# First chunk of a one-core trunk layer: q summed while h is made, k and v taken forward, modulation sums on ScalarE

## The chip, the cores and the metric

One core of one Trainium2 chip runs the whole kernel in one launch; the host only lays the arrays out. The metric is the device time in microseconds (us). Engines are named as in the profile: PE is TensorE (PEld its weight loads), DVE VectorE, ACT ScalarE, POOL GpSimd, and SP SyncE, which here issues every DMA.

## The reference

One layer on 2048 tokens of width 1024, in float32:

```python
mod = silu(c) @ w_ada + b_ada
shift, scale, gate = split(mod)                  # 1024 each
h = rms_norm(x, norm_g) * (1 + scale) + shift
u = h @ w_in                                     # 1024 x 5632
glu_in, gate_a, q, k, v, gate_b, m_a, m_b = split(u)
y_a = conformer_conv_branch(glu_in, gate_a, ...) # GLU, causal depthwise conv 31, LayerNorm, swish, proj
q = head_rms_norm(q, q_gain); k = head_rms_norm(k, k_gain)   # 8 heads x 64
o = stick_breaking_attention(q, k, v)
y_b = (o * silu(gate_b)) @ w_sb_out
y = sigmoid(m_a) * y_a + sigmoid(m_b) * y_b
x = x + gate * (y @ w_out)
```

The changed part makes `h`, the columns of `w_ada` for shift and scale, and `q`, `k`, `v` of the first chunk.

## The kernel before

The tokens lie reversed, and are worked on in four chunks of 512 in the order 3, 2, 1, 0 (`ORDER`). Every large product is made of three float32r matmuls (high part by high part, high by low, low by high), so each weight and each activation is split: ScalarE copies the high part (`whi`, `hhi`), and GpSimd or VectorE subtracts it for the low part (`wlo`, `hlo`). A weight panel of 128 x 1024 comes in two halves of 128 x 512 through the two-buffer tile `wl` (`split_into`, lines 105 to 111): DMA, ScalarE copy, subtraction, for which GpSimd is the default.

**h of a chunk.** `xn_pair` (line 329) loads two blocks of 128 tokens, sums squares on ScalarE, computes a reciprocal root in ten small VectorE steps (`rsqrt`) and scales `xt` on VectorE (line 342). `x_block` transposes 128 x 128 pieces on TensorE (line 127). `modulate` (line 353) then makes `hf` = scale * x + shift on ScalarE (line 359), the high part on ScalarE for the first chunk and on VectorE for the others (lines 364 and 366), and the low part on GpSimd or VectorE (line 367). `h_half` does this for half a chunk.

**The first chunk (chunk 3).** For each of the eight 128-row slices of the model width, `mod_col` (line 225) multiplies two rows-blocks of `w_ada` with silu(c) and sums them on VectorE, two one-element VectorE sums add the bias and the gain (lines 408 and 410, `b_s` and `a_s`), and the slice of h is made. Right behind it go the matmuls of this slice into the PSUM tiles of q, heads 0 to 3 (group 0). Those of group 1 (heads 4 to 7) come after, from weights kept in tiles `w1h` and `w1l`. Then h of chunks 2, 1 and 0 is made, and q of group 0 of these chunks is begun.

**q, k and v.** There are six groups of four heads: 0 and 1 are q, 2 and 3 k, 4 and 5 v. `nat_tile` makes one half (256 tokens) of a group in a chunk: 2 token blocks x 8 slices x 3 = 48 matmuls of 128 x 256 into a `pd` PSUM tile, of which there are five. For q and k, ScalarE squares each head with a running sum (line 272), `head_norm` computes the root on VectorE and scales into `qn` (line 287), and `transposed` turns two heads at a time on TensorE, splits the result into `qhi` and `qlo` (one buffer each, lines 306 and 307, k at 302 and 303) and stores four pieces. For v, `v_store` splits (lines 318 and 319) and stores eight pieces.

**What sets the order.** A scheduler orders each engine's instructions by priority in program order, within dependences and buffers; each engine then runs its list in order, and SP issues the DMAs in order too. From the first `glu` on, TensorE's order is pinned. The depthwise convolution's 204 VectorE steps wait in a list; after each output tile `tick` gives out `RATE` of them (2.6), as well as the norms and transposes put off by `later`. The q and k transposes take `qhi` and `qlo` from the pool `cvp`, which is opened after all h is made; so those of the first chunk's q wait until then. All of k is made in `qk_group(2, True)` and `qk_group(3, True)`, v in `v_block(4)` and, in the LayerNorm stage, `v_group(5)`, in which each tile also moves the LayerNorm one step on (`next(ln)`). Attention follows, with the merge gates as filler on TensorE, and then the output projection.

Of the kernel before, what the change touches and what calls it, by code (L numbers as in the profile page):

```python
# [8 lines left out]
F32 = mybir.dt.float32  # L9
# [9 lines left out]
P = 128  # L19
SEQ = 2048  # L20
D = 1024
# [11 lines left out]
NXT = 7  # L33
NWA = 4
RATE = 2.6
# [15 lines left out]
def trunk_kernel(  # L51
# [130 lines left out]
    with ExitStack() as s1:  # L182
# [74 lines left out]
        def qk_group(grp, isk, chunks=ORDER, w2=None, ps0=None):  # L257

            w2 = w2 or ps0 or [piece(w_qkv[grp, i]) for i in range(2)]
            h4 = (grp % 2) * 4  # L260
            dst = kst_d if isk else qst_d
            for b in chunks:
# [3 lines left out]
                for half in range(2):  # L266
                    ps = ps0[half] if ps0 else nat_tile(pd, w2, b, half)
# [25 lines left out]
        def transposed(qn, pr, dst, h4, b, isk):  # L293
# [5 lines left out]
            hi = cvp.tile([P, CH], F32R, tag="qhi", name="qhi", bufs=1)  # L299
            lo = cvp.tile([P, CH], F32R, tag="qlo", name="qlo", bufs=1)  # L300
# [13 lines left out]
        def v_store(ps, st, h4, b, half):  # L314
# [7 lines left out]
            for i in range(4):  # L322
                nc.sync.dma_start(vst_d[h4 + i][b][:, 2 * half:2 * half + 2, :], s2[:, i])

# [51 lines left out]
        with tc.tile_pool(name="hx", reuse_waits="tile", bufs=1) as hx:  # L376
            g0 = ORDER[0]
            w2_q1 = [(hx.tile([P, D], F32R, name=f"w1h{i}"), hx.tile([P, D], F32R, name=f"w1l{i}"))
                     for i in range(2)]
# [6 lines left out]
            for o in range(0, D, CH):  # L386
# [5 lines left out]
            xs += xn_pair(4 * g0 + 2, hx, NXT, True)  # L392
            ba = load_const(b_ada, 24, "ba")
            ng = load_const(norm_g, KC, "ng")
            ba1 = sm.tile([P, KC], F32, name="ba1", bufs=1)
            nc.vector.tensor_scalar(out=ba1, in0=ba[:, KC:2 * KC], scalar1=1.0, scalar2=None,
                                    op0=ALU.add)
            w2_q0 = []
            qk_ps = [[pd.tile([P, 2, 256], F32, tag="pd", name="pd") for _ in range(2)]
                     for _ in range(2)]  # L400
            for kc in range(KC):
                for j in (8 + kc, kc):
                    mod_col(j, ca, hx.tile([P, D], F32, tag="wa", name="wa", bufs=NWA))
                if kc < 2:
                    w2_q0.append(load_piece(wpa, w_qkv[0, kc]))
                elif kc in (4, 5):
                    split_into(w_qkv[1, kc - 4], *w2_q1[kc - 4])
                nc.vector.tensor_tensor(out=b_s[:, kc:kc + 1], in0=mod[:, kc:kc + 1],
                                        in1=ba[:, kc:kc + 1], op=ALU.add)
                nc.vector.scalar_tensor_tensor(out=a_s[:, kc:kc + 1], in0=mod[:, 8 + kc:9 + kc],  # L410
                                               scalar=ba1[:, kc:kc + 1], in1=ng[:, kc:kc + 1],
                                               op0=ALU.add, op1=ALU.mult)
                modulate(x_block(xs, kc), hx.tile([P, CH], F32, tag="hf", name="hf", bufs=6),
                         g0, 0, kc, (1, 1),
                         nc.gpsimd if kc < KC - 1 else nc.vector)
                for half in range(2):
                    for i in range(2):
                        nat_mm(qk_ps[0][half], w2_q0, g0, half, i, kc,
                               kc == 0 and i == 0, kc == KC - 1 and i == 1)
            for kc in range(KC):  # L420
                for half in range(2):
                    for i in range(2):
                        nat_mm(qk_ps[1][half], w2_q1, g0, half, i, kc,
                               kc == 0 and i == 0, kc == KC - 1 and i == 1)
            for o in (0, 2):
                h_half(ORDER[1], o, hx, NXT, ())
            qk_group(0, False, ORDER[:1], ps0=qk_ps[0])
            for o in (0, 2):
                h_half(ORDER[2], o, hx, NXT, (0, 4))
            qk_group(1, False, ORDER[:1], ps0=qk_ps[1])  # L430
# [3 lines left out]
        with tc.tile_pool(name="hz", reuse_waits="tile", bufs=1) as hz:  # L434
# [6 lines left out]
            gain = load_const(q_gain, 1, "gain")  # L441
            gk = load_const(k_gain, 1, "gk")
            nc.vector.tensor_tensor(out=gain, in0=gain, in1=gk, op=ALU.mult)


        with tc.tile_pool(name="cvp", reuse_waits="tile", bufs=2, side="right") as cvp:
# [121 lines left out]
            qk_group(1, False, ORDER[1:])  # L568
            silu_block(B_GA + 1, ga_d[1])
            glu(2)  # L570
            qk_group(2, True)
            v_block(4)
            glu(3)
            qk_group(3, True)
# [521 lines left out]
```

## Time and profile before

| | |
|---|---|
| runs | 1952.85, 1944.73, 1953.7 us (median 1952.85) |
| profiled execution | 1947.37 us, span 1945.6 us, mean granted clock 0.993 |
| PE busy over the span | 94% |
| first glu matmul | 136.46 us after the start |
| last TensorE wait ahead of the dense stage ends | 157.4 us |
| first attention matmul | 825.4 us |
| data moved | 206.88 MB |

A row of a timeline gives start, length, engine, line of the kernel, operation, output and inputs by the program's names, shapes and, in brackets, the idle time before it with what ended it. A row of waits gives who waited for whom, the total in us, the number of waits and the longest. L12 is line 12 of the kernel before.

### The profile page before, as it was taken

What the parts mean: (1) busy time and instruction counts of PE and PEld (TensorE: products, weight loads), DVE (VectorE), ACT (ScalarE), POOL (GpSimd) and SP (SyncE); (2) the same over time, 40 slices, a digit from 0 to 9 for tenths busy, and PEclk for the clock granted to TensorE, in tenths of its full rate; (3) what the DMA queues carried; (4) which work ended last, traced back from release to release, by engine and by line L of the source; (5) the groups of instructions that cost most, each with busy time, mean ns of one, the idle gap of its engine ahead of it and who ended that gap; (6) DMA issues with size and microseconds to landing.
All of it is one profiled execution on the core that took longest, in us unless ns stands there. A gap on an engine that the chain in (4) does not pass through costs nothing.

```text
span 1945.6 us, 27211 instructions
## 1 busy us (share of the span) xinstructions
PE 1823.4 (94%) x9612; PEld 1517.2 (78%) x9612; DVE 1248.5 (64%) x1947; ACT 809.5 (42%) x1988; POOL 667.6 (34%) x739
## 2 busy tenths in 40 slices
PE   5889999999999989999998999999989889999999
PEld 4777898998988977777776777676767667888887
DVE  6864678787787445267776767676777797333341
ACT  3761122231221122266666666666667664010100
POOL 6441111011011144356465656455655551010100
PEclk9999999999999999999999999999999999999999
DMA  7335114052142444423232323131313246453532
GB/s 246 135 107 176 43 28 136 17 167 78 45 140 71 152 146 156 145 90 88 62 89 63 92 66 91 57 95 58 103 55 101 69 152 205 138 153 101 162 97 77
DMA packets 115290, 206.88 MB, mean 106 GB/s; under 512 B 15185, under 2 KB 27473, under 8 KB 115154
## 3 DMA queue, kind: packets, MB, share of 16 engines
q1 hardware_dynamic: 115154, 205.14, 33.8%
q8 instruction: 76, 1.25, 0.3%
q14 instruction: 60, 0.49, 0.1%
HBM read 133.78 MB, written 71.30 MB: 105 GB/s over the span
## 4 chain that ended last, share of the span: by engine, by line
PE 59%; DVE 16%; POOL 11%; issue 6%; DMA 5%; ACT 3%; SPq 1%; DVEq 0%; POOLq 0%; ACTq 0%
PE pd L122 33%; PE po L122 9%; POOL w L818 7%; PE p L122 7%; DVE sc L811 6%; PE av L122 4%; PE pT L127 3%; PE z L122 3%; DVE tlo L843 2%; POOL wlo L110 1%; DVE sc L815 1%; DMA gt<-ga 1%; ACT z L806 1%; DVE hhi L366 1%; DMA wl<-in_w_out_dram 1%
## 5 line engine op out<-in xcount | busy, mean ns | idle before, releaser
L818 POOL TENSOR_TENSOR w<-w,sc 128x512 f32<-128x512 f32 (+1 forms) x320 | 361.5, 1131 | 328.6 <-DVE sc L811 243.3
L122 PE MATMUL pd<-hhi,whi 128*128 128x512 f32 x1024 | 411.9, 402 | 0.0
L122 PE MATMUL pd<-hhi,wlo 128*128 128x512 f32 x1024 | 402.3, 393 | 0.0
L122 PE MATMUL pd<-hlo,whi 128*128 128x512 f32 x1024 | 401.7, 392 | 0.0
L110 POOL TENSOR_TENSOR wlo<-wl,whi 128x512 fp32r<-128x512 f32 x92 | 135.6, 1484 | 462.4 <-ACT whi L109 462.1
L811 DVE TENSOR_TENSOR_SCAN sc<-z,sc,w 128x512 f32<-128x512 f32 x192 | 244.0, 1276 | 53.1 <-ACT z L806 52.5
L805 ACT ACTIVATE w<-z 128x512 f32<-128x512 f32 (+1 forms) x320 | 171.8, 537 | 142.9 <-PE z L122 117.9
L122 PEld LDWEIGHTS pd<-hhi,wlo 128*128 128x128 f32 x1024 | 193.0, 189 | 41.9
L122 PE MATMUL pd<-whi,hhi 128*128 128x256 f32 x736 | 214.9, 292 | 8.1 <-DVE qn L287 8.1
L122 PEld LDWEIGHTS pd<-hhi,whi 128*128 128x128 f32 x1024 | 195.2, 191 | 33.8
L122 PE MATMUL pd<-whi,hlo 128*128 128x256 f32 x736 | 213.0, 291 | 8.5 <-POOL hlo L367 8.3
L122 PEld LDWEIGHTS pd<-hlo,whi 128*128 128x128 f32 x1024 | 193.6, 189 | 34.3
L122 PE MATMUL pd<-wlo,hhi 128*128 128x256 f32 x736 | 212.6, 289 | 0.2 <-POOL wlo L110 0.2
L122 PE MATMUL z<-kt,q 128*128 128x512 f32 (+2 forms) x640 | 195.9, 387 | 12.3 <-DVE sc L811 10.1
L842 ACT CAST thi<-pT 128x512 fp32r<-128x512 f32 (+1 forms) x320 | 165.1, 526 | 92.1 <-PE pT L127 88.7
L843 DVE TENSOR_TENSOR tlo<-pT,thi 128x512 fp32r<-128x512 f32 (+1 forms) x320 | 184.5, 596 | 13.4 <-ACT thi L842 11.0
L127 PE MATMUL pT<-ident,w 128*128 128x128 f32 x1088 | 174.8, 275 | 12.3 <-POOL w L818 12.1
L127 PEld LDWEIGHTS pT<-ident,w 128*128 128x128 f32 x1088 | 137.1, 140 | 49.3 <-POOL w L818 19.6
L806 ACT ACTIVATE z<-z 128x512 f32<-128x512 f32 (+1 forms) x320 | 171.5, 536 | 0.0
L122 PE MATMUL av<-tlo,vt 128*128 128x512 f32 (+1 forms) x320 | 126.1, 394 | 34.3 <-DVE tlo L843 30.5
L122 PEld LDWEIGHTS pd<-whi,hlo 128*128 128x128 f32 x736 | 143.8, 196 | 11.8 <-POOL hlo L367 11.2
L122 PEld LDWEIGHTS pd<-whi,hhi 128*128 128x128 f32 x736 | 144.9, 197 | 9.2 <-DVE qn L287 8.5
(274 smaller groups left out, 2994.3 us busy)
## 6 DMA issues: line engine op xcount, KB each, us to landing
wl<-in_w_in_dram SPq DMA_DIRECT2D x64, 256.0 KB, 2.9
wa<-in_w_ada_dram SPq DMA_DIRECT2D x24, 512.0 KB, 5.6
xt<-in_x_n_dram SPq DMA_DIRECT2D x16, 512.0 KB, 5.9
vst<-st SPq DMA_DIRECT2D x64, 128.0 KB, 1.9
kt<-kst SPq DMA_DIRECT2D x32, 256.0 KB, 2.8
vt<-vst SPq DMA_DIRECT2D x32, 256.0 KB, 2.8
q<-qst SPq DMA_DIRECT2D x32, 256.0 KB, 2.9
q<-qst SPq DMA_DIRECT2D x64, 128.0 KB, 3.1
```

What stands on the lines that cost most here:

```text
L110: (lo_eng or nc.gpsimd).tensor_tensor(out=lo[:, s], in0=wl, in1=f(hi[:, s]), op=ALU.subtract)
L122: i = nc.tensor.matmul(*a, **k)
L127: i = nc.tensor.transpose(*a)
L366: nc.vector.tensor_copy(hi, hf)
L805: nc.scalar.activation(out=w[:, lo:], in_=z[:, lo:], func=AF.Sigmoid, scale=HD ** -0.5)
L806: nc.scalar.activation(out=z[:, lo:], in_=z[:, lo:], func=AF.Sigmoid, scale=-HD ** -0.5)
L811: nc.vector.tensor_tensor_scan(out=s[:, 1:], data0=z, data1=w, initial=s[:, 0:1], op0=ALU.mult, op1=ALU.bypass)
L815: nc.vector.tensor_tensor_scan(out=s[:, lo + 1:], data0=z[:, lo:], data1=tri[:, :CH - lo], initial=1.0, op0=ALU.mult, op1=ALU.max)
L818: nc.gpsimd.tensor_tensor(out=w[:, lo:], in0=w[:, lo:], in1=s[:, lo:CH], op=ALU.mult)
L842: nc.scalar.copy(out=thi[:, :n], in_=pT[:, :n])
L843: nc.vector.tensor_tensor(out=tlo[:, :n], in0=pT[:, :n], in1=f(thi[:, :n]), op=ALU.subtract)
```

## The change

For the first chunk, both q groups are summed slice by slice while its h is made. Their norms no longer go through `qk_group` but through a new function `norm_at_once`, which squares a whole 128 x 512 PSUM tile on ScalarE, sums it by heads with one VectorE reduce, and runs `head_norm` and both transposes at once, with `qhi` and `qlo` in the pool `hx`. Then come k of the first chunk (groups 2 and 3) and its v (groups 4 and 5), each with its weights loaded for this use alone, between the four half chunks of h of chunks 2 and 1. Later, k and v of the other three chunks are made with the weights loaded a second time. The sums `a_s` and `b_s` are ScalarE instructions. `NXT`, the buffers for x blocks, goes from 7 to 6, and `RATE` from 2.6 to 2.9. `gain` is loaded at the start.

```diff
-NXT = 7
+NXT = 6
-RATE = 2.6
+RATE = 2.9
+        def norm_at_once(pss, grp, b, pool):
+
+            ssq = sm.tile([P, 4, 4], F32, tag="ssq", name="ssq")
+            qn = qp.tile([P, 4, 4, HD], F32, tag="qn", name="qn", bufs=2)
+            for half in range(2):
+                sq = pool.tile([P, CH], F32, tag="sqv", name="sqv", bufs=1)
+                nc.scalar.activation(out=sq, in_=pss[half].rearrange("p t c -> p (t c)"),
+                                     func=AF.Square)
+                nc.vector.tensor_reduce(
+                    out=ssq[:, 2 * half:2 * half + 2].rearrange("p t h -> p (t h)"),
+                    in_=sq.rearrange("p (n d) -> p n d", d=HD), axis=AX.X, op=ALU.add)
+            head_norm(pss, ssq, qn)
+            for pr in range(2):
+                transposed(qn, pr, kst_d if grp >= 2 else qst_d, (grp % 2) * 4, b, grp >= 2, pool)
...
-            w2_q1 = [(hx.tile([P, D], F32R, name=f"w1h{i}"), hx.tile([P, D], F32R, name=f"w1l{i}"))
-                     for i in range(2)]
+            def hx_piece(src, tag, lo_eng=None):
+                hi = hx.tile([P, D], F32R, tag=tag, name="whx", bufs=4)
+                lo = hx.tile([P, D], F32R, tag=tag, name="wlx", bufs=4)
+                split_into(src, hi, lo, lo_eng)
+                return hi, lo
...
-            nc.vector.tensor_scalar(out=ba1, in0=ba[:, KC:2 * KC], scalar1=1.0, scalar2=None,
-                                    op0=ALU.add)
-            w2_q0 = []
+            nc.vector.scalar_tensor_tensor(out=ba1, in0=ba[:, KC:2 * KC], scalar=1.0, in1=ng,
+                                           op0=ALU.add, op1=ALU.mult)
+            w2_q0, w2_q1 = [], []
...
                 if kc < 2:
-                    w2_q0.append(load_piece(wpa, w_qkv[0, kc]))
-                elif kc in (4, 5):
-                    split_into(w_qkv[1, kc - 4], *w2_q1[kc - 4])
-                nc.vector.tensor_tensor(out=b_s[:, kc:kc + 1], in0=mod[:, kc:kc + 1],
-                                        in1=ba[:, kc:kc + 1], op=ALU.add)
-                nc.vector.scalar_tensor_tensor(out=a_s[:, kc:kc + 1], in0=mod[:, 8 + kc:9 + kc],
-                                               scalar=ba1[:, kc:kc + 1], in1=ng[:, kc:kc + 1],
-                                               op0=ALU.add, op1=ALU.mult)
+                    i = kc
+                    w2_q0.append(load_piece(wpa, w_qkv[0, i]))
+                    w2_q1.append(hx_piece(w_qkv[1, i], "w1"))
+                col = slice(kc, kc + 1)
+                nc.scalar.activation(out=a_s[:, col], in_=mod[:, 8 + kc:9 + kc],
+                                     func=AF.Identity, scale=ng[:, col], bias=ba1[:, col])
+                nc.scalar.activation(out=b_s[:, col], in_=mod[:, col], func=AF.Identity,
+                                     bias=ba[:, col])
...
+                for ps2, w2 in zip(qk_ps, (w2_q0, w2_q1)):
+                    for half in range(2):
+                        for i in range(2):
+                            nat_mm(ps2[half], w2, g0, half, i, kc,
+                                   kc == 0 and i == 0, kc == KC - 1 and i == 1)
+            def first(grp, tag, lo_eng=None):
+                w2 = [hx_piece(w_qkv[grp, i], tag, lo_eng) for i in range(2)]
+                return [nat_tile(pd, w2, g0, half) for half in range(2)]
+
+            norm_at_once(qk_ps[0], 0, g0, hx)
+            k0 = first(2, "wa")
+            h_half(ORDER[1], 0, hx, NXT, ())
+            norm_at_once(qk_ps[1], 1, g0, hx)
+            k1 = first(3, "w1")
+            h_half(ORDER[1], 2, hx, NXT, ())
+            norm_at_once(k0, 2, g0, hx)
+            for grp, tag in ((4, "wa"), (5, "w1")):
+                ps2 = first(grp, tag, nc.vector if grp == 4 else None)
                 for half in range(2):
...
-            for o in (0, 2):
-                h_half(ORDER[1], o, hx, NXT, ())
-            qk_group(0, False, ORDER[:1], ps0=qk_ps[0])
-            for o in (0, 2):
-                h_half(ORDER[2], o, hx, NXT, (0, 4))
-            qk_group(1, False, ORDER[:1], ps0=qk_ps[1])
+                    v_store(ps2[half], qp.tile([P, D], F32, tag="qn", name="st", bufs=2),
+                            (grp % 2) * 4, g0, half)
+                h_half(ORDER[2], 2 * (grp - 4), hx, NXT, (0, 4))
+                if grp == 4:
+                    norm_at_once(k1, 3, g0, hx)
...
-                for b in ORDER:
+                for b in ORDER[1:]:
...
-            qk_group(2, True)
+            qk_group(2, True, ORDER[1:])
...
-            qk_group(3, True)
+            qk_group(3, True, ORDER[1:])
```

On TensorE, where the transposes of chunk 2's x begin (`xt`; `hhi_3` and `hlo_3` are h of the first chunk, `hhi_2` and `hlo_2` of the second), the list of the kernel before has the matmuls of q group 0 on chunk 2 between them:

```order
L127 MATMUL pt<-ident,xt 128x128 x8
L122 MATMUL pd<-whi,hhi_2_317 128x256
L122 MATMUL pd<-wlo,hhi_2_317 128x256
L127 MATMUL pt<-ident,xt 128x128 x2
L122 MATMUL pd<-whi,hlo_2_325 128x256
L122 MATMUL pd<-whi,hhi_2_318 128x256
```

And in the changed kernel, at the same transposes (`whx` and `wlx` are weights of k):

```order
L127 MATMUL pt<-ident,xt 128x128 x4
L122 MATMUL pd<-whx,hhi_3_301 128x256
L122 MATMUL pd<-wlx,hhi_3_301 128x256
L122 MATMUL pd<-whx,hlo_3_309 128x256
L122 MATMUL pd<-whx,hhi_3_302 128x256
L122 MATMUL pd<-wlx,hhi_3_302 128x256
L122 MATMUL pd<-whx,hlo_3_310 128x256
L127 MATMUL pt<-ident,xt 128x128 x2
```

Matmuls that need h of chunk 2, which is just being made, are replaced there by matmuls of k on the first chunk, whose h is complete.

On SP, the stores of the first chunk's q (`qst_3`) stand in the kernel before behind all loads of x:

```order
L108 DMA wl<-in_w_in_dram 128x512 x2
L334 DMA xt<-in_x_n_dram 128x1024 x4
L448 DMA ca<-in_c_dram 128x1024
L311 DMA qst_3_102<-qhi 64x512
L312 DMA qst_3_102<-qlo 64x512
```

In the changed kernel, loads of k and v weights (`w_qkv`) and of x stand between these stores:

```order
L312 DMA qst_3_122<-qlo 64x512
L108 DMA wl<-in_w_qkv_dram 128x512 x2
L311 DMA qst_3_126<-qhi 64x512
L311 DMA qst_3_130<-qhi 64x512
L312 DMA qst_3_126<-qlo 64x512
L312 DMA qst_3_130<-qlo 64x512
L108 DMA wl<-in_w_qkv_dram 128x512 x2
L349 DMA xt<-in_x_n_dram 128x1024
L311 DMA kst_3_70<-qhi 64x512
```

The weights of v and some blocks of x are thus issued only once the stores ahead of them have their data.

On SP at the end of the convolution, the two stores of its last channels (`cv_166`) stand in the kernel before behind the last gate store (`gb_3`):

```order
L545 DMA gb_2_189<-sg 128x512
L108 DMA wl<-in_w_in_dram 128x512 x2
L545 DMA gb_3_190<-sg 128x512
L497 DMA cv_166<-cc 128x1024
L503 DMA cv_166<-cb 128x1024
```

In the changed kernel they stand ahead of the last two:

```order
L534 DMA cv_166<-cb 128x1024
L528 DMA cv_166<-cc 128x1024
L576 DMA gb_2_189<-sg 128x512
L108 DMA wl<-in_w_in_dram 128x512
L576 DMA gb_3_190<-sg 128x512
```

The convolution's last results are stored two gate tiles earlier.

28 lines of the change are left out of this document (10 added, 18 removed).

## The prediction

> **What bounds the kernel now.** I read the page first, then the busy time by stretch, the waits of the first 166 us, and the timeline there engine by engine. The page:
>
> ```profile
> PE 1823.4 (94%) x9612; PEld 1517.2 (78%) x9612; DVE 1248.5 (64%) x1947; ACT 809.5 (42%) x1988; POOL 667.6 (34%) x739
> ```
>
> TensorE is the bound over the whole, so moving its work pays only where it is idle. The table by stretch says where (columns: stretch, its length, then busy us of PE, PEld, DVE, ACT, POOL with counts, granted clock, DMA share, GB/s):
>
> ```profile
> 0.00:40.00 40.00, 20.53 (x84) 15.84 (x85) 29.37 (x53) 16.91 (x27) 22.93 (x31) 1.00 0.72 250
> 40.00:60.00 20.00, 16.65 (x135) 16.04 (x135) 12.04 (x25) 8.46 (x16) 9.97 (x6) 1.00 0.87 318
> 60.00:80.00 20.00, 13.62 (x93) 11.16 (x92) 19.16 (x49) 17.32 (x71) 12.15 (x16) 0.93 0.26 81
> 80.00:100.00 20.00, 17.84 (x128) 16.83 (x128) 17.90 (x52) 13.76 (x75) 9.28 (x12) 0.90 0.22 79
> 100.00:120.00 20.00, 16.32 (x118) 13.97 (x118) 18.68 (x62) 14.53 (x51) 7.79 (x10) 1.00 0.04 11
> 120.00:140.00 20.00, 15.20 (x101) 14.24 (x100) 10.11 (x25) 9.25 (x45) 7.13 (x9) 0.91 0.47 130
> 140.00:160.00 20.00, 16.49 (x77) 13.19 (x76) 6.39 (x18) 7.11 (x10) 2.58 (x2) 0.98 0.68 190
> 166.00:633.00 467.00, 465.96 (x2777) 416.10 (x2776) 351.13 (x430) 106.66 (x461) 67.07 (x44) 1.00 0.28 86
> ```
>
> From 166 to 633 us TensorE is busy 465.96 of 467. In the seven rows before, it is busy 116.65 of 160, with the granted clock down to 0.90 to 0.93 in three of them. VectorE is the full engine there from 60 to 120 us (55.74 of 60), and the waits say whose results TensorE lacks:
>
> ```profile
> PE pd L122 <- DVE qn L287: 8.1, 2, 5.1
> PE pt L127 <- DVE qn L287: 3.4, 1, 3.4
> PE pt L127 <- DVE qlo L307: 2.6, 1, 2.6
> PE pt L127 <- DVE qry L85: 2.2, 1, 2.2
> ACT hf L359 <- DVE b_s L408: 23.8, 7, 7.6
> DVE wa L225 <- DMA wa<-in_w_ada_dram: 10.0, 3, 4.7
> ```
>
> **The change part by part.** *TensorE work moved, -46.1 us.* One half of a group in a chunk (256 tokens) is 48 matmuls; where TensorE runs freely the chain of waits has
>
> ```profile
> 282.16 5.76 PE pd L122 x48
> ```
>
> k and v of the first chunk are four groups of two such halves: 8 x 5.76 = 46.1 us. Six leave the 465.96 us, two the LayerNorm stage. They go ahead of 166 us, so the question is what that stretch grows by.
>
> *VectorE in that stretch.* Its h work runs from the first to the last of these rows, 65 us:
>
> ```profile
> 58.29 0.17 DVE L338 TENSOR_SCALAR ss<-ss 128x2 f32<-128x2 f32 x1 [0.36 <-ACT sq L336]
> 98.17 0.71 DVE L282 TENSOR_SCALAR qv<-ssq 128x16 f32<-128x16 f32 x1
> 101.48 1.29 DVE L287 TENSOR_TENSOR qn<-pd,qry 128x512 f32<-128x512 f32 x2
> 122.86 0.41 DVE L367 TENSOR_TENSOR hlo<-hf,hhi 128x256 fp32r<-128x256 f32 x1
> 123.87 0.68 DVE L307 TENSOR_TENSOR qlo<-pt,qhi 128x512 fp32r<-128x512 f32 x1
> ```
>
> The last row is the first `lo` of a head transpose, so all eight of the first chunk's (four q, four k) now come ahead of the last chunk's h. Added: two k norms at 98.17 to 102.77 = 4.6 us each, 9.2; eight `lo` at 0.69, 5.5; four v splits at the same pass length, 2.8; four weight remainders given to VectorE (group 4), 2.8. The eight tensor_reduce sums of squares occur nowhere in before; between the 0.17 us small pass and the 1.29 us two-pass row I take the 0.69 us of a 128x512 pass, which they are in length: 5.5 (1.4 to 10.3). That is 25.8 us. The 32 ScalarE squares that they replace free ScalarE, which is not full.
>
> *Twelve weight remainders more on GpSimd.* A pass takes
>
> ```profile
> 142.06 1.29 POOL L110 TENSOR_TENSOR wlo<-wl,whi 128x512 fp32r<-128x512 f32 x1 [2.07 <-ACT whi L109]
> ```
>
> so 15.5 us. What that does to VectorE shows at 63 us, where the same sort of two-element operation takes 0.15 us alone and 0.72 us beside a GpSimd pass, ending with it:
>
> ```profile
> 63.17 0.15 DVE L98 TENSOR_TENSOR nxt<-nxt,ss 128x2 f32<-128x2 f32 x1
> 63.33 0.73 POOL L367 TENSOR_TENSOR hlo<-hf,hhi 128x256 fp32r<-128x256 f32 x1 [8.58 <-DVE nxt L98]
> 63.36 0.72 DVE L99 SCALAR_TENSOR_TENSOR nxy<-nxt,nxy 128x2 f32<-128x2 f32 x1
> ```
>
> Over the whole stretch, the groups by line (mean ns of one after the busy time):
>
> ```profile
> L366 DVE CAST hhi<-hf 128x256 fp32r<-128x256 f32 x48 | 23.4, 531 | 1.4 <-ACT hf L359 1.4
> L367 POOL TENSOR_TENSOR hlo<-hf,hhi 128x256 fp32r<-128x256 f32 x40 | 31.1, 800 | 36.0 <-DVE nxy L99 21.2 <-DVE nxt L98 8.9 <-DVE hhi L366 5.7
> ```
>
> The 48 casts of h average 0.53 us, against 0.28 for one alone (row in the next fence): 48 x 0.25 = 12 us. Normalisations and small passes such as that at 63.36 lose time too, an estimated 5 us. That is 17 us lost beside 31.1 us of GpSimd passes, 0.55 of them. So 0.55 x 15.5 = 8.5 us more (0 to 15.5). VectorE's stretch grows by 25.8 + 8.5 = **34.3 us**.
>
> ```profile
> 64.00 0.28 DVE L366 CAST hhi<-hf 128x256 fp32r<-128x256 f32 x1
> 22.21 1.22 DVE L225 SCALAR_TENSOR_TENSOR wa<-wa,ca 128x1024 f32<-128x1024 f32 x1
> 22.49 2.06 POOL L367 TENSOR_TENSOR hlo<-hf,hhi 128x512 fp32r<-128x512 f32 x1 [3.49 <-ACT hhi L364]
> 23.47 1.10 DVE L408 TENSOR_TENSOR b_s<-mod,ba 128x1 f32<-128x1 f32 x1
> ```
>
> In the last three rows the engines take turns: the GpSimd pass lasts until 24.55, long after the VectorE row that started before it ended at 23.43, and the sum over one element, 1.10 us, ends at 24.57. The Trainium skill, "SBUF — State Buffer", in its part on the port that VectorE and GpSimd share, calls this an exclusive lock for the whole instruction. The trace agrees at these rows. By that rule the 8.5 would be 15.5 and the sum below -14.8 instead of -21.8; it is the second rival.
>
> *Modulation sums on ScalarE, -5 us.* The two groups of sums leave VectorE:
>
> ```profile
> L408 DVE TENSOR_TENSOR b_s<-mod,ba 128x1 f32<-128x1 f32 x8 | 7.0, 869 | 0.2
> L410 DVE SCALAR_TENSOR_TENSOR a_s<-mod,ba,ng 128x1 f32<-128x1 f32 x8 | 5.3, 660 | 0.2
> ```
>
> So 12 us at most would go from the first chunk. But VectorE also waited 10.0 us there for w_ada, whose loads stand in one queue between weight loads, and the second q group's weights now come earlier in it. I take 5 us (0 to 12); ScalarE waited 23.8 us for these sums and has room.
>
> *The backlog after the last chunk, -7 us.* The first chunk's q transposes now stand in the h stretch, so after it queue 6 pairs instead of 10. The `lo` of these pairs come one at a time, since their buffer waits for its store:
>
> ```profile
> 129.79 0.69 DVE L307 TENSOR_TENSOR qlo<-pt,qhi 128x512 fp32r<-128x512 f32 x1
> 153.66 0.69 DVE L307 TENSOR_TENSOR qlo<-pt,qhi 128x512 fp32r<-128x512 f32 x1 [3.00 <-DMA qst<-qlo]
> ```
>
> five intervals in 23.87 us, 4.8 each. The three waits of 3.4, 2.6 and 2.2 us sit here, with some 4 us of slower clock after them: 12 us at most; I take 7.
>
> *New waits in order, +4 us.* The same single buffers now stand inside the h stretch: ScalarE waits for a store with h's evictions queued behind it, and SP holds k and v weight loads behind q stores. Other rows lie between in each queue, so 4 us (0 to 23, worked out under the third rival).
>
> *LayerNorm stage, -2 us.* The convolution steps are given out 2.9 per tile, so the last of them stand ahead of the last two gate tiles, no longer behind them; now the first LayerNorm matmul waits
>
> ```profile
> PE mub L122 <- ACT hl L635: 3.2, 1, 3.2
> 787.02 1.05 PE L122 MATMUL psb<-dg,ones 128*128 128x128 f32 x8
> 809.47 0.32 SPq L688 DMA_DIRECT2D za<-lsg  x1
> 820.73 0.59 SPq L780 DMA_DIRECT2D q<-qst  x1
> 825.42 0.49 PE L122 MATMUL z<-kt,q 128*128 128x512 f32 x1 [0.58 <-DMA q<-qst]
> ```
>
> 3.2 us, which goes. Against it, the LayerNorm's steps are called once a tile and two tiles are gone: the first z came 38.4 us after the last spread, and now has 48 matmuls (half of 96 x 0.228, 10.9 us) less between. The last store at +22.5, the loads of k and q and their landing (4.7 us from issue to z) come to about 28 us against 27.5: a wait of 1 to 3 us. Bounds -5 to +4. VectorE's higher rate costs nothing: with 351 us of work in 467 it has 116 us spare, and 35 us less leaves 81.
>
> **The sum**: -46.1 + 34.3 - 5 - 7 + 4 - 2 = -21.8 us. The profiled run took 1947.4 us (span 1945.6), so 1925.6, rounded to **1926**. The median of the runs is 1952.85, 5.5 above that run; I add nothing for it.
>
> **The rivals.** *VectorE's additions hide too* (16 in 100): it is busy only 16.5 of 40 us from 120 to 160, so 23.5 us of the 34.3 could fall into that room if the order let h go first. Then -46.1 + 10.8 - 5 + 4 - 2 = -38.3: 1909. Against it: the k norms stand ahead of the last chunk's h in the code.
>
> *GpSimd's passes cost VectorE their full length* (15): -21.8 + 7 = -14.8: 1933. For it: the turns at 22 and 63 us. Against: sums and splits that read PSUM mix in, and only 0.55 was lost so far.
>
> *The single buffers pace the stretch* (9): the four k pairs add 4 x 4.8 = 19 us that nothing covers, so waits of 23 instead of 4: -2.8, 1945, no difference.
>
> *Slower* (5): one queue alternates stores and weight loads, and each of the sixteen half panels of k and v waits for the one before. With two buffers and 4.8 us for load, copy and remainder, that is 16 x 2.4 = 38 us on top of VectorE's 34.3: -46.1 + 34.3 + 38 - 5 - 2 = +19: 1967. It decides once such waits pass some 34 us.
>
> **How the numbers follow.** The forecast has 55 in 100. About 0.5%, 9.8 us, can be told from no change: faster is below 1943.1, slower above 1962.6. Forecast, first and second rival lie below, 86 in 100, and one of the third's nine, which lies at the border: faster 87. The other eight are the same, and the last rival's 5 are slower. The range takes, downward, no cost of turns and the whole 12 us at the start (-15.5, and on to the first rival at 1909), upward full turns, no gain at the start and 5 us more of waits in order (+17): **1909 to 1943**.
>
> **What would show it.** Right: VectorE above 90% from 55 to about 150 us, the first glu matmul some 24 us later than now with nearly no idle TensorE after it, reduces near 0.69 us, no wait of mub. Wrong: ScalarE or SP waiting for stores beyond 10 us, weights as the releaser of TensorE in the k or v pieces, a DVE gap there, or TensorE idle between 170 and 600 us.

## The result and the profile after

The changed kernel takes 1932.13 us (median of 4 runs, 1930.69 to 1933.59) beside 1952.48 for the kernel before: a ratio of 0.9904 (95% interval 0.9877 to 0.9931). The forecast was 1926, within 1909 to 1943. Its profiled run took 1933.59 us with a span of 1931.8, so against the profiled run of before the span fell by 13.8 us where the sum said 21.8. Two executions of experiments, the profiled one of e7 and one of e10, took 6258.87 and 6255.30 us and are left out, so e7 is told by its times alone.

The page and the table by stretch of the changed kernel (same columns as in the prediction):

```profile
PE 1820.2 (94%) x9612; PEld 1515.8 (78%) x9612; DVE 1252.1 (65%) x1943; ACT 815.9 (42%) x1900; POOL 686.3 (36%) x751
```

```profile
0.00:40.00 40.00, 22.79 (x109) 17.15 (x109) 21.94 (x39) 19.13 (x36) 23.01 (x33) 1.00 0.71 252
40.00:60.00 20.00, 16.23 (x130) 15.68 (x131) 13.74 (x20) 13.00 (x26) 10.25 (x7) 1.00 0.77 262
60.00:80.00 20.00, 14.53 (x97) 13.92 (x96) 19.58 (x66) 9.98 (x19) 7.05 (x6) 0.83 0.63 193
80.00:100.00 20.00, 18.63 (x154) 17.79 (x153) 17.96 (x42) 13.74 (x28) 9.46 (x12) 1.00 0.59 170
100.00:120.00 20.00, 17.29 (x135) 16.67 (x134) 16.37 (x42) 10.10 (x19) 12.06 (x15) 0.93 0.58 167
120.00:140.00 20.00, 19.98 (x165) 19.69 (x165) 6.59 (x13) 8.20 (x26) 5.08 (x7) 0.98 0.67 205
140.00:160.00 20.00, 17.13 (x129) 16.36 (x128) 17.21 (x54) 14.71 (x59) 9.43 (x14) 0.91 0.10 34
160.00:180.00 20.00, 20.00 (x152) 19.13 (x151) 7.54 (x22) 8.86 (x54) 3.34 (x3) 1.00 0.22 62
200.00:600.00 400.00, 400.00 (x2345) 355.76 (x2344) 323.08 (x380) 92.30 (x383) 70.08 (x42) 1.00 0.28 87
```

From 160 us on TensorE is full, as forecast. But VectorE is the full engine only from 60 to 80 us. From 120 to 140 it is busy 6.59 of 20 while TensorE is full, and from 140 to 160 both are below 17.3. No engine paces the stretch alone.

To measure the stretch I use one place, the 97th glu matmul: it opens the fifth glu tile, from where on TensorE is full. It starts at 165.63 us in before; in the changed kernel:

```profile
158.24 0.42 DVE L382 TENSOR_TENSOR hlo<-hf,hhi 128x256 fp32r<-128x256 f32 x1
175.43 0.48 PE L122 MATMUL pd<-hhi,whi 128*128 128x512 f32 x1
199.06 0.48 PE L122 MATMUL pd<-hhi,whi 128*128 128x512 f32 x1
```

The rows are the last of h, the first glu matmul and the 97th. (The expectations of e1 to e4 give 175.67 and 199.31 for the last two, a quarter of a microsecond late.) The glu begins 39.0 us later than the 136.46 of before, not the forecast 24. The 97th is 33.4 us later. With the 46.1 us of k and v matmuls that are gone behind it, the front has won 12.7 us and the rest of the span 1.1.

A second place is the first attention matmul, where all the changed work is done. It starts at 825.42 us in before; in the changed kernel, in e6 (the change without k and v) and in e4 (twelve passes moved from GpSimd to VectorE):

```profile
809.20 0.50 PE L122 MATMUL z<-kt,q 128*128 128x512 f32 x1
```

```profile
811.59 0.49 PE L122 MATMUL z<-kt,q 128*128 128x512 f32 x1
```

```profile
802.86 0.50 PE L122 MATMUL z<-kt,q 128*128 128x512 f32 x1
```

From there to the end the three kernels and before do the same 5110 matmuls, and still take 1122.6, 1120.6, 1120.5 and, in before, 1120.2 us. No run shows why, so two spans that differ by a few microseconds are compared at this place as well.

In front of the 97th glu matmul, time is TensorE's busy time plus its idle time. From 40 us to the 97th glu matmul the three tables of before, of e6 and of the changed kernel have one row each:

```profile
40.00:165.63 125.63, 101.76 (x667) 89.96 (x666) 86.20 (x229) 70.78 (x260) 48.91 (x54) 0.95 0.43 138
```

```profile
40.00:152.18 112.18, 95.41 (x639) 84.65 (x640) 86.89 (x235) 69.47 (x208) 45.96 (x52) 0.95 0.50 156
```

```profile
40.00:158.66 118.66, 102.45 (x786) 98.76 (x787) 90.32 (x228) 68.85 (x167) 53.22 (x57) 0.94 0.56 173
158.66:199.06 40.40, 40.40 (x255) 36.27 (x254) 18.32 (x49) 16.65 (x72) 7.83 (x7) 1.00 0.45 134
40.00:199.06 159.06, 142.85 (x1039) 135.03 (x1040) 108.64 (x275) 85.50 (x236) 61.05 (x64) 0.96 0.53 163
```

TensorE idled 125.63 - 101.76 = 23.87 us in before, 16.77 in e6 and 16.21 in the changed kernel. Between the last two, 46.88 us of time were added for 47.44 us of busy TensorE: k and v found 0.6 us of idle time to lie in (1.5 us when the count begins at 0, since some of the added work lies ahead of 40 us). At the first attention matmul the changed kernel is 2.4 us ahead of e6, where the sum gave k and v 15.3. That is the finding of this study, and the experiments follow it from several sides.

### The profile page after: what moved, and what is told of

The parts are those of the page before. It is cut to its first block, busy times and chain, and to the rows that moved or that the text cites. A ratio compares the mean times of both kernels' runs of the same rounds, so it can differ in the third digit from the quotient of the medians.

```text
span 1931.8 us, 27158 instructions
## 1 busy us (share of the span) xinstructions
PE 1820.2 (94%) x9612; PEld 1515.8 (78%) x9612; DVE 1252.1 (65%) x1943; ACT 815.9 (42%) x1900; POOL 686.3 (36%) x751
## 3 DMA queue, kind: packets, MB, share of 16 engines
q8 instruction: 76, 1.25, 0.3%
## 4 chain that ended last, share of the span: by engine, by line
PE 64%; DVE 13%; POOL 10%; issue 6%; DMA 3%; ACT 3%; SPq 0%; DVEq 0%; POOLq 0%; ACTq 0%
PE pd L122 36%; PE po L122 9%; POOL w L849 7%; PE p L122 7%; DVE sc L842 6%; PE av L122 4%; PE pT L127 3%; PE z L122 3%; DVE tlo L874 2%; DVE sc L846 1%; PE pt L127 1%; ACT z L837 1%; POOL wlo L110 1%; DMA gt<-ga 1%; DMA wa<-in_w_ada_dram 1%
## 5 line engine op out<-in xcount | busy, mean ns | idle before, releaser
L110 POOL TENSOR_TENSOR wlo<-wl,whi 128x512 fp32r<-128x512 f32 x92 | 140.2, 1534 | 406.3 <-ACT whi L109 406.1
L874 DVE TENSOR_TENSOR tlo<-pT,thi 128x512 fp32r<-128x512 f32 (+1 forms) x320 | 184.5, 596 | 13.8 <-ACT thi L873 11.5
L122 PE MATMUL pd<-whi,hlo 128*128 128x256 f32 x608 | 172.8, 286 | 6.0 <-POOL hlo L382 5.9
L122 PE MATMUL pd<-whi,hhi 128*128 128x256 f32 x608 | 174.8, 288 | 1.7 <-DVE sg L575 1.7
L122 PE MATMUL pd<-wlo,hhi 128*128 128x256 f32 x608 | 173.0, 285 | 0.0
L122 PE MATMUL av<-tlo,vt 128*128 128x512 f32 (+1 forms) x320 | 126.1, 394 | 35.4 <-DVE tlo L874 31.2
L122 PEld LDWEIGHTS z<-kt,q 128*128 128x128 f32 x640 | 107.7, 189 | 42.0 <-DVE sc L842 24.4
L846 DVE TENSOR_TENSOR_SCAN sc<-z,tri 128x512 f32<-128x512 f32 (+3 forms) x128 | 104.2, 818 | 48.4 <-ACT z L837 38.2
```

Source lines behind the costliest of these rows:

```text
L110: (lo_eng or nc.gpsimd).tensor_tensor(out=lo[:, s], in0=wl, in1=f(hi[:, s]), op=ALU.subtract)
L122: i = nc.tensor.matmul(*a, **k)
L846: nc.vector.tensor_tensor_scan(out=s[:, lo + 1:], data0=z[:, lo:], data1=tri[:, :CH - lo], initial=1.0, op0=ALU.mult, op1=ALU.max)
L874: nc.vector.tensor_tensor(out=tlo[:, :n], in0=pT[:, :n], in1=f(thi[:, :n]), op=ALU.subtract)
```

## The experiments

Theory H: the last chunk's x rows come late and leave VectorE a hole. Theory T: VectorE and GpSimd take turns, and the weight remainders on GpSimd pace the stretch. Theory B: the single q and k buffers pace it.

### e1, the x rows in a pool of their own

```diff
-                h_half(ORDER[3], o, hz, 4, (6, 7))      # hz opened on the memory that hx leaves
+                h_half(ORDER[3], o, hz, NXT, (6, 7))    # hz: xt, sq, hf of all chunks, on the right
```

> The x rows, their squares and hf of all chunks stand in a pool of their own, so the last chunk's x rows can be loaded into the next free x buffer instead of into memory that the v weights still hold. Nothing else is changed. The last chunk's loads were issued at 132.70 us, VectorE was busy 6.59 of 20 us from 120 to 140 us, and TensorE 17.13 of 20 at a granted clock of 0.91 from 140 to 160. Theory H (the hole: that load is what is late): the loads are issued before 115 us, VectorE is above 12 of 20 us from 120 to 140, the first glu matmul (175.67) and the start of the fifth glu tile (199.31) come some 4 us earlier (2 to 7; TensorE has no more idle time there to give back), and the whole is 1928 us. Theory T (turns with GpSimd set the pace of the stretch) and theory B (single q and k buffers and their stores set it): the loads move but the fifth glu tile starts within 1.5 us of 199.31, and the whole stays at 1932.

1931.64 us, ratio 0.9909 (0.9882 to 0.9935). The last loads of x rows (start, issue time) and the table, of the changed kernel's loads first and then of e1:

```profile
132.70 2.92 SPq L349 DMA_DIRECT2D xt<-in_x_n_dram  x4
```

```profile
118.09 0.90 SPq L349 DMA_DIRECT2D xt<-in_x_n_dram  x2
```

```profile
100.00:120.00 20.00, 15.83 (x122) 15.45 (x121) 19.17 (x50) 10.81 (x20) 10.66 (x12) 0.91 0.67 194
120.00:140.00 20.00, 19.33 (x152) 17.62 (x150) 15.56 (x35) 12.95 (x25) 8.95 (x13) 1.00 0.65 188
140.00:160.00 20.00, 19.63 (x159) 18.94 (x159) 12.41 (x29) 9.89 (x57) 6.49 (x11) 1.00 0.01 5
```

The hole is filled (15.56 of 20) and TensorE's idle time from 140 to 160 goes from 2.87 to 0.37 us. But from 100 to 120 it is busy 15.83 where it was 17.29. The 97th glu matmul starts at 197.27, 1.8 us earlier. H is right about what was late and wrong about its worth: the idle time moved ahead. The whole can't be told from the changed kernel's 1932.13.

### e2, two buffers for split q and k

```diff
-            hi = (pool or cvp).tile([P, CH], F32R, tag="qhi", name="qhi", bufs=1)
+            hi = (pool or cvp).tile([P, CH], F32R, tag="qhi", name="qhi", bufs=2 if pool else 1)
```

The same for `qlo`, with hf at four buffers.

> The split q and k of the first chunk have two buffers each instead of one; hf has four instead of six to make room. Theory B: VectorE's waits for the split in the first 200 us (qlo after qhi 14.3 us in 4) fall below 6, and the fifth glu tile starts 3 to 6 us before 199.31. Theories H and T: within 1.5 us of 199.31, since VectorE's and TensorE's own work and the late x rows are unchanged; with hf at four possibly 1 to 2 us later.

1934.05 us, ratio 0.9921 (0.9891 to 0.9951), the 97th glu matmul at 199.49. VectorE's wait in the first 200 us, of the changed kernel and of e2:

```profile
DVE qlo L307 <- ACT qhi L306: 14.3, 4, 5.5
```

```profile
DVE qlo L308 <- ACT qhi L307: 14.1, 4, 5.5
```

A second buffer leaves the wait as it was, so it is not for a buffer: VectorE waits for ScalarE to come to the split. ScalarE's own waits for the stores, 5.1 us before q's splits and 3.1 before k's in the changed kernel, are gone in e2, and the 97th glu matmul is no earlier. B falls, up to the 1 to 2 us that the smaller `hf` may have cost.

### e3, the modulation sums back on VectorE

```diff
-                nc.scalar.activation(out=b_s[:, col], in_=mod[:, col], func=AF.Identity,
-                                     bias=ba[:, col])
+                nc.vector.tensor_tensor(out=b_s[:, col], in0=mod[:, col], in1=ba[:, col], op=ALU.add)
```

The same for `a_s`.

> The sixteen modulation sums of one column are back on VectorE, as in the kernel before; the rest is the changed kernel. The prediction priced their move at 5 us of the first chunk (0 to 12). With that price right, the first chunk's last remainder (54.56 us) comes at 59 to 60 us, the fifth glu tile some 5 us later than 199.31 and the whole at 1937. If the transfer of w_ada sets that stage (VectorE waited 12.0 us in 9 for it), the last remainder comes at 55 to 57 us and the whole at 1932 to 1934.

1932.67 us, ratio 0.9911 (0.9884 to 0.9938), the 97th glu matmul at 199.67, 0.6 us later. The groups of the modulation products up to 60 us (count, busy, mean ns, idle before) are, in the changed kernel and in e3:

```profile
L225 DVE SCALAR_TENSOR_TENSOR wa<-wa,ca 128x1024 f32<-128x1024 f32 x16 | 25.2, 1598 | 8.8 <-DMA wa<-in_w_ada_dram 8.7
```

```profile
L225 DVE SCALAR_TENSOR_TENSOR wa<-wa,ca 128x1024 f32<-128x1024 f32 x16 | 19.9, 1246 | 4.5 <-DMA wa<-in_w_ada_dram 4.4
```

In the changed kernel, what the sums leave free is taken by products that are 0.35 us longer (5.3 us in all) and by 4.3 us more of waiting for w_ada. The last row of the first chunk starts 2.1 us later in e3 (56.62, and 54.56 in the changed kernel), and 0.6 us of that is left at the 97th matmul. The move is worth 0.6 us, not 5.

### e4 and e8, fewer and more GpSimd passes

```diff
             def first(grp, tag, lo_eng=None):
+                lo_eng = nc.vector                                            # e4
...
+                nc.gpsimd.tensor_tensor(out=junk, in0=hi[:, s], in1=hi[:, s], op=ALU.subtract)   # e8
```

e4 takes the twelve remainder passes of k and v off GpSimd; e8 keeps them and adds twelve whose result nothing reads (`hf` has five buffers there instead of six).

> All sixteen weight remainders of the k and v pieces of the first chunk run on VectorE (0.68 us each), where twelve ran on GpSimd (1.33 us each). VectorE gains 12 x 0.68 = 8.2 us of work, GpSimd loses 16. Theory T (VectorE loses what a GpSimd pass beside it takes, about 1 us at each of twelve passes, seen as one-column steps of 1.2 us): the small steps of the norms fall from means of 0.31 to 0.35 us to about 0.18, VectorE's busy time up to 160 us grows by no more than 2 us, and the fifth glu tile starts within 2 us of 199.31 or earlier. If the passes cost VectorE little, its busy time grows by 7 to 8 us and the fifth glu tile starts 3 to 6 us later, the whole at 1935 to 1938. Theories H and B say nothing of the small steps.

> The changed kernel with each of the twelve weight-remainder passes of the k and v pieces on GpSimd followed by a second GpSimd pass of the same size into a tile that nothing reads (hf has five buffers to make room). Nothing waits for the second pass but GpSimd's own next one, and GpSimd was busy some 9 of 20 us there. Theory T: twelve more passes of 1.3 us take 0.5 to 1 us each from VectorE, so the 97th glu matmul comes 5 to 10 us after 199.06 and the whole at 1937 to 1942. If the passes cost VectorE nothing and e4 gained from something else (earlier weights, fewer waits on SP), it comes within 2 us of 199.06 and the whole at 1932 to 1934.

e4: 1925.76 us, ratio 0.9876 (0.9851 to 0.9901), the 97th glu matmul at 193.04, 6.0 us earlier. e8: 1938.33 us, ratio 0.9938 (0.9920 to 0.9956), at 205.18, 6.1 us later. The table to the end of h, e4 and then e8 (the changed kernel's row, 118.66, is above):

```profile
40.00:152.74 112.74, 101.41 (x793) 97.98 (x793) 88.48 (x242) 68.29 (x168) 39.62 (x45) 0.95 0.59 183
```

```profile
40.00:166.13 126.13, 104.20 (x798) 99.67 (x799) 101.02 (x230) 70.86 (x173) 66.75 (x68) 0.95 0.54 166
```

In e4 VectorE took over twelve passes (its sixteen take 12.0 us, the four of the changed kernel 2.7), and its busy time fell from 90.32 to 88.48. In e8 it has no work more, and is busy 101.02. Why shows in the rows of the changed kernel around 60 us, VectorE's and GpSimd's:

```profile
59.50 1.25 DVE L98 TENSOR_TENSOR nxt<-nxt,ss 128x2 f32<-128x2 f32 x1
60.78 1.21 DVE L99 SCALAR_TENSOR_TENSOR nxy<-nxt,nxy 128x2 f32<-128x2 f32 x1
62.03 0.16 DVE L96 SCALAR_TENSOR_TENSOR nxt<-nxy 128x2 f32<-128x2 f32 x1
```

```profile
59.45 2.53 POOL L110 TENSOR_TENSOR wlx<-wl,whx 128x512 fp32r<-128x512 f32 x2 [3.02 <-ACT whx L109]
```

Two passes end at 61.98; beside each, VectorE gets through one step of two elements, which alone takes 0.16 us. From 55 to 160 us the groups of such steps (mean ns after the busy time) in the changed kernel and in e4 are

```profile
L98 DVE TENSOR_TENSOR nxt<-nxt,ss 128x2 f32<-128x2 f32 x18 | 5.6, 310 | 0.4
L99 DVE SCALAR_TENSOR_TENSOR nxy<-nxt,nxy 128x2 f32<-128x2 f32 x18 | 4.5, 248 | 0.4
L96 DVE SCALAR_TENSOR_TENSOR qrt<-qry 128x16 f32<-128x16 f32 x14 | 4.8, 346 | 0.2
```

```profile
L98 DVE TENSOR_TENSOR nxt<-nxt,ss 128x2 f32<-128x2 f32 x18 | 3.3, 186 | 0.3
L99 DVE SCALAR_TENSOR_TENSOR nxy<-nxt,nxy 128x2 f32<-128x2 f32 x18 | 3.3, 186 | 0.3
L96 DVE SCALAR_TENSOR_TENSOR qrt<-qry 128x16 f32<-128x16 f32 x16 | 4.8, 302 | 0.2
```

T holds as a cost: one edit and its opposite move the time by the same 6 us in opposite directions. That GpSimd merely finishes its own work later in e8 doesn't explain it: TensorE's waits for GpSimd in this stretch are 4.8 us in the changed kernel and 4.4 in e8, those for VectorE 8.7 and 14.4. The small-step forecast holds in part: the steps of the x norms fall to 0.19 us, those of the q and k norms stay at 0.30; the GpSimd passes that are left in e4 are h's own.

e4 also limits the finding: with the passes on VectorE, k and v do bring something. At the first attention matmul e4 is 8.7 us ahead of e6.

### e5, both

> The two edits of e1_x_rows_free and e4_remainders_on_vector together: x rows in a pool of their own, and all sixteen weight remainders of the k and v pieces on VectorE. They brought the 97th glu matmul (the start of the fifth glu tile) from 199.06 to 197.27 and to 193.04 us. If turns and late x rows are separate losses they add up: the 97th glu matmul at 191 us and the whole at 1924 (1922 to 1926). If VectorE's time is now the bound of the stretch, filling its hole with the last chunk's x rows gives more than before: 187 to 190, the whole at 1920 to 1922. If TensorE has no idle time left to give, 193 and 1926.

1925.70 us, ratio 0.9877 (0.9858 to 0.9895), the 97th glu matmul at 191.98: the two nearly add up at that place (1.1 us beyond e4, and e1 alone won 1.8), and the whole can't be told from e4.

### e6, q without k and v

```diff
-RATE = 2.9
+RATE = 2.6
-            k0 = first(2, "wa")          # likewise k1, both v pieces and their norms and stores
-            for b in ORDER[1:]:          # v_block, v_group, qk_group(2), qk_group(3)
+            for b in ORDER:
```

> Only the q part of the change: k and v of the first chunk stay with the other chunks behind the glu, the convolution steps go at 2.6 a tile as before; q of both groups is summed, normed and split at once and the modulation sums are on ScalarE. This computes the same as both kernels. By the prediction's terms this part is worth + 2.7 (four reduces) + 2.8 (four splits) - 5 (sums) - 7 (backlog) = -6.5 us against the kernel before, so some 1944 beside a median of 1950.7, and moving k and v brings the other 12 to 16 us. With the sums worth 0.6 us (as e3_sums_on_vector showed) it is -2: 1948. If it comes at 1936 or below, the gain is in q and k and v bring nothing.

1932.05 us, ratio 0.9904 (0.9886 to 0.9923): the whole gain, without k and v. h ends at 122.72 us, 0.5 before that of before, and the rows from there to the 97th glu matmul are, in before and in e6:

```profile
123.27:165.63 42.36, 34.85 (x177) 29.68 (x177) 15.19 (x40) 15.91 (x51) 7.79 (x7) 0.92 0.60 168
```

```profile
40.00:122.72 82.72, 66.41 (x484) 60.05 (x485) 71.95 (x201) 56.55 (x172) 37.39 (x45) 0.94 0.46 149
122.72:152.18 29.46, 28.99 (x157) 24.60 (x157) 14.93 (x35) 12.91 (x38) 8.56 (x7) 1.00 0.60 175
```

The tail behind h is 12.9 us shorter, and TensorE is nearly full in it at a granted clock of 1.00 instead of 0.92. Counted from 0 to the 97th glu matmul, TensorE's idle time falls by 8.4 us (43.3 to 35.0), and its busy time by 5.1 for the same matmuls (122.29 to 117.22): not the whole gain is idle time filled. Both outcomes that I had priced for q, 1944 and 1948, were far off, and the third line of the expectation (1936 or below) is what came.

### e9, q and v without k

```diff
-            k0 = first(2, "wa")          # likewise k1 and the two k norms
-RATE = 2.9
+RATE = 2.75
```

> The changed kernel without its k part: k of the first chunk stays with the other chunks behind the glu, v stands where the change put it, the convolution steps go at 2.75 a tile. This computes the same as both kernels. In e6_q_only the 97th glu matmul started at 152.18 us and the whole took 1932. If VectorE paces the stretch (the prediction), v costs its splits 2.8, its remainders 2.8 and a share of four GpSimd passes, 6 to 8 us, for 23 us of matmuls taken from the dense stage: the 97th glu matmul at 158 to 161 and the whole at 1915 to 1919. If TensorE has no room in the stretch and the two engines wait for one another, v costs what it weighs: 173 to 177, the whole at 1930 to 1934. Between them, the cost of k (its norms and splits on VectorE) is what eats the gain of v: 165 to 168, 1923 to 1926.

1931.56 us, ratio 0.9891 (0.9869 to 0.9914). The table:

```profile
40.00:135.58 95.58, 84.51 (x625) 78.15 (x626) 73.58 (x205) 60.96 (x165) 42.84 (x49) 0.95 0.53 170
40.00:170.39 130.39, 119.32 (x831) 108.83 (x832) 87.61 (x239) 75.69 (x220) 50.69 (x56) 0.96 0.51 162
```

From e6 to e9 the 97th glu matmul moves by 18.2 us for v's four halves of 5.76, 23.0: v is ahead by 4.8 there, and TensorE's idle time falls from 16.77 to 11.07. From e9 to the changed kernel it moves by 28.7 for k's 23.0: k is behind by 5.6, and the idle time is back at 16.21. VectorE's busy time to the end of h grows by 1.6 us for v (71.95 to 73.58) and by 16.7 for k (to 90.32). At this place the result lies between two of my cases, 165 to 168 (k's norms eat the gain of v) and 173 to 177 (TensorE has no room); the whole time is that of the second. Behind the 97th matmul e9's span is 3.2 us longer than the halves account for (1760.2 where 1780.0 - 23.0 = 1757.0). That comes after the changed work: at the first attention matmul (806.32) e9 is still 5.3 us ahead of e6, and its attention takes 1124.3 us where e6's takes 1120.6. So v alone wins in the stretch and the whole doesn't show it; why the attention takes longer is open.

### e10, e6 with the split late

```diff
             for pr in range(2):
-                transposed(qn, pr, ...)
+                later(1 + 2 * grp + pr, lambda pr=pr: transposed(qn, pr, qst_d, grp * 4, b, False))
```

> e6_q_only with one thing undone: q of the first chunk is summed and normed at once as there, but transposed and split a few half tiles later, in turn with the other chunks' q, as in the kernel before. If the gain of e6 (97th glu matmul from 165.63 to 152.18) is the shorter backlog of transposes after the last chunk, most of it goes: 160 to 165, the whole at 1940 to 1946. If it comes from the squares (one reduction in place of sixteen small activations) and from the second group's matmuls beside the first's, it stays: 152 to 155, 1932 to 1935.

1944.97 us, ratio 0.9959 (0.9942 to 0.9977), the 97th glu matmul at 158.51.

```profile
40.00:117.15 77.15, 65.53 (x461) 58.34 (x461) 69.22 (x193) 52.82 (x156) 36.59 (x45) 0.96 0.36 128
117.15:158.51 41.36, 33.55 (x179) 28.39 (x179) 15.41 (x40) 15.91 (x51) 7.80 (x7) 0.96 0.63 175
```

The long tail is back, 41.36 us beside 29.46, while h ends 5.6 us earlier without the splits in its way. The place lies between the two forecasts: the backlog is worth 11.9 us in the tail and costs 5.6 ahead of it. The other 7.1 us from before to e10 come from the rest of the q part (sums of squares at once, the second group's matmuls beside the first's, the x buffers and the earlier load of `gain` included), which was not taken apart. Behind that place e10's span is 3.5 us longer than e6's (1783.5 against 1780.0), 2.6 of them ahead of the first attention matmul; no run shows why.

### e7, e11 and e12, versions with all remainders on VectorE

```diff
-                    w2_q0.append(load_piece(wpa, w_qkv[0, i]))
+                    w2_q0.append(load_piece(wpa, w_qkv[0, i], nc.vector))     # and w2_q1
```

e7 is e4 with this, e12 is e5 with it, e11 is q and v alone with it and with e1's pool, v beside the second chunk's h.

> e4_remainders_on_vector, and the eight remainders of the two q groups' weights, made in the first 40 us beside the modulation products, on VectorE as well: no weight remainder of the first 130 us is left on GpSimd. Theory T holds there too (products of 1.60 us in the mean, 1.2 alone), so the products get shorter; but if the transfer of w_ada sets that stage, the first chunk's last remainder stays at 54 to 56 us and the 97th glu matmul within 1.5 us of 193.04, the whole at 1925 to 1927. If VectorE sets it, the first chunk comes 2 to 5 us earlier with the glu, the whole at 1921 to 1923; if VectorE is then overfull, it comes 2 to 4 us later.

> q and v of the first chunk as in e9_q_and_v, but v stands beside the second chunk's h instead of the third's, x rows in a pool of their own and every weight remainder up to there on VectorE, those of q too. If k's norms are what costs, this is the fastest: 1912 to 1918. If TensorE's room is what is short, it comes out as e12_all_tuned, 1920 to 1924.

> e5_both and e7_q_remainders_too together: q, k and v of the first chunk, x rows in a pool of their own, all weight remainders of the first 130 us on VectorE. They took 1925.7 and 1923.4 us. If the first chunk comes earlier without GpSimd's passes (theory T beside the modulation products), the first chunk's last remainder is at 50 to 53 us, the 97th glu matmul at 188 to 190 and the whole at 1919 to 1922; if the transfer of w_ada holds it, 54 us, 191.5 to 192.5 and 1924 to 1926.

e7: 1921.37, 1922.03 and 1924.80 us in its three timed runs, ratio 0.9858 (0.9839 to 0.9877). e11: 1930.60, ratio 0.9882 (0.9855 to 0.9909), the 97th glu matmul at 167.87. e12: 1928.02, ratio 0.9874 (0.9848 to 0.9900), at 191.98, exactly where e5 has it although its first chunk ends earlier. The last row of the first chunk in e5 and in e12:

```profile
54.21 0.69 DVE L382 TENSOR_TENSOR hlo<-hf,hhi 128x512 fp32r<-128x512 f32 x1
```

```profile
52.27 0.69 DVE L382 TENSOR_TENSOR hlo<-hf,hhi 128x512 fp32r<-128x512 f32 x1
```

Its end comes 1.9 us earlier and nothing comes of it later. e11 was to be the fastest if k's norms are what costs, and like e12 if TensorE's room is short; by the whole it is like e12, later than the 1920 to 1924 named for that case, though at the first attention matmul e12, with k, is 4.6 us ahead (802.97 and 807.57). e4, e5, e7 and e12 cannot be told from one another by their intervals. All four lie below both kernels. e4's runs, 1925.14 to 1926.06, lie below the changed kernel's 1930.69 to 1933.59, though in another series, and the intervals of the two ratios overlap; the traces agree, with the first attention matmul 6.3 us earlier. One line of code is all that it needs.

## Why the forecast came out right, point by point

The time came out within its range, and the sum is wrong in its parts, so the agreement is in good part luck. On its own base, the profiled run of before, the sum said 21.8 us and the profiled runs differ by 13.8; that the medians differ by 20.4 comes mostly from a profiled run of before that was 5 us faster than the median. 1932.13 is also nearer to the second rival's 1933 than to the forecast. The terms for q (+2.7 reduces, +2.8 splits, -5 sums, -7 backlog) made -6.5; e6 measured -13.4 (spans 1945.6 and 1932.2). The terms for k and v made the other -15.3; from e6 to the changed kernel the span moved by -0.4, and the first attention matmul by -2.4.

**TensorE work moved, -46.1.** Right as an amount: behind the 97th glu matmul the span falls from 1780.0 to 1732.7, in which k's sixteen head transposes are moved too, some 1.4 us that the term left out (four of them take 0.36 us in the dense stage of before). The step that failed is the next one: "They go ahead of 166 us, so the question is what that stretch grows by." I let VectorE's added time answer that, as if TensorE had the room. But time up to the 97th matmul is TensorE's busy plus its idle time, and of the latter q left 16.77 us for 46.1 us of matmuls. It could have been read from the table of before: 23.87 us idle from 40 to 165.63 bound what moved matmuls can win there while each takes the same busy time, and the forecast would have needed nearly all of it. What had been running in that room were the later chunks' q matmuls. They now queue behind h: the tail after the last row of h is 40.40 us in the changed kernel, all TensorE, beside 29.46 in e6.

**VectorE, +34.3.** h ends 158.66 - 123.27 = 35.4 us later, so the number looks met, but it isn't made of what I added up. VectorE's busy time from 40 us to the end of h grew by 90.32 - 71.01 = 19.3, not 34.3. What I had listed came in part: the reduces took 0.68 us where I took 0.69, and the eight `lo` (5.7 us), the splits of v (2.8) and the four remainders (2.7) came as priced. But of the two norms that I added only one is there: the `qn` rows ahead of the end of h go from six to eight, as a norm of a later chunk's q went behind it. The groups of the changed kernel from 55 to 160 us:

```profile
L333 DVE TENSOR_REDUCE ssq<-sqv 128x8 f32<-128x512 f32 x8 | 5.4, 679 | 2.4 <-ACT sqv L331 2.4
L381 DVE CAST hhi<-hf 128x256 fp32r<-128x256 f32 x48 | 17.5, 391 | 1.6 <-ACT hf L374 1.4
L319 DVE TENSOR_TENSOR st<-pd,st 128x512 fp32r<-128x512 f32 x4 | 2.8, 688 | 8.8 <-ACT st L318 8.8
```

The casts of h became shorter (17.5 us in all, 23.4 before), a gain of 5.9 us that I had not counted; 29 of the 48 now run beside a GpSimd pass, 38 did before. In exchange the stretch holds time in which VectorE waits: 8.8 us for ScalarE's copies of v's tiles alone, which in their turn wait for TensorE, and more for late x rows. The row of ScalarE's wait:

```profile
ACT st L318 <- PE pd L122: 6.7, 3, 5.2
```

TensorE waits in the same stretch 7.3 us for VectorE's `qn`. So the engines wait for one another: e1 fills VectorE's hole and TensorE's idle time only moves.

**Turns with GpSimd.** Taken at 0.55 of 15.5 us, 8.5. By e8, twelve passes of 1.08 us (12.9 in all) add 10.7 us of busy VectorE, 0.83 of them, and 6.1 us to the whole path; by e4, taking twelve away wins 6.0 although VectorE has twelve passes more. The second rival's full length was nearer. The Trainium skill, "SBUF — State Buffer", in its part on the shared port, says that the one that starts first gets the port pair for its whole instruction; the rows at 59.50 and 60.78 agree.

**Modulation sums, -5.** Worth 0.6 (e3): longer products and the wait for w_ada take most of what the sums leave free.

**Backlog, -7.** -11.9 in the tail, +5.6 in the stretch (e10), where I had 2.8 for the splits: the mechanism right, both sizes too small, and the waits of TensorE in the tail are gone.

**New waits, +4.** Not the buffers (e2). The last x rows waited for memory that v's weights held, which was not in the term; it is worth 1.8 us (e1).

**LayerNorm stage, -2.** Met in size: from the 97th glu matmul to the first attention matmul the time falls from 659.8 to 610.1 us, and 46.1 of k and v and 1.4 of transposes leave 2.1. But e6 and e10, which do the same work there, differ by 2.6 in the same stretch, so these 2.1 alone show little. The attention behind it took 2.4 us longer, so over all that follows the 97th glu matmul -1.1 is left. The `mub` wait of 3.2 us is gone, that for `t` is a little shorter and one for `dg` is new (before, then the changed kernel):

```profile
PE pst L122 <- DVE t L614: 9.3, 3, 6.4
```

```profile
PE pst L122 <- DVE t L645: 7.1, 2, 4.9
PE psb L122 <- DVE dg L651: 2.3, 1, 2.3
```

Of the signs named beforehand, no idle TensorE from 170 to 600, the reduces and `mub` came out right; VectorE above 90% to 150 us and the glu 24 us later were wrong. Of the signs against the forecast two came: the gap of VectorE, and SP standing more than 10 us at q's stores (18.6 us in six waits for ScalarE's splits, the longest 14.8). Weights held TensorE up for 0.6 us only.

## What to carry to other kernels

Work that is moved to where the bound engine idles can win no more than the idle time there, as long as it takes the same busy time: write down that engine's busy and idle time up to a fixed place, before and after, and ask which waits the move removes. A second engine's added time says nothing about it while the two wait for one another. And a sum that comes out right is no proof of its terms: leaving out k and v showed that the part of the change that was to bring 15 us brought between 0.4 and 2.4, until twelve passes beside it were moved to another engine.

## What the runs showed of the hardware

A GpSimd pass of 128 x 512 takes 1.3 us, the same pass on VectorE 0.68 (0.78 in the mean of e4's sixteen), and beside each of the two GpSimd passes at 59.45 us VectorE got through one step of two elements, 1.25 us where 0.16 is usual. Moving twelve passes to VectorE, busy 90.32 of 118.66 us, made it less busy (88.48 us) and the kernel 6 us shorter.
